# A row softmax: whole-tile passes, stores on Pool's queue, four tiles summed by DVE, instruction streams aligned

## Chip, cores, metric

One core of one Trainium2 chip. The metric is the device time of the kernel in microseconds; lower is better. "Landing" of a transfer is the last of the 16 semaphore updates that the trace has for it (512 for the 32 transfers of before). "Before" is the given kernel, "after" the changed one.

## The reference

```python
batch, seq, dim = 32, 512, 1024            # x is float32, temperature 0.5
scaled = x / temperature
shifted = scaled - np.max(scaled, axis=-1, keepdims=True)
exp_x = np.exp(shifted)
return (exp_x / np.sum(exp_x, axis=-1, keepdims=True)).astype(np.float32)
```

16384 rows of 1024 float32: 67.11 MB are read and 67.11 MB are written.

## The kernel before

Sixteen tiles of 128 partitions x 8 rows x 1024 elements (4 MiB), six buffers. SP issues loads, ACT issues stores; a load waits until the store that last used its buffer has landed (224.5 us in 10 waits, in the trace). Work goes in groups of four rows, two groups a tile, and DVE divides a group only after the maximum of the next one.

```python
TILES = [[8]] * 16
BUFS = 6
GROUP = 4
# ... (cut: pools, the list of groups)
def load():
    i = len(tiles)
    if i < len(TILES):
        xt = data.tile([P, sum(TILES[i]), d], f32, name="xt")
        nc.sync.dma_start(out=xt, in_=dram(xf, i))
        tiles.append(xt)

def maximum(g):            # DVE: top over 4 rows, bias = -scale * top
    ...
def exponential(g):        # ACT: one instruction per row, with its sum
    for b in range(k):
        nc.scalar.activation(row, row, Exp, bias=bias[:, b : b + 1], scale=scale,
                             accum_out=sums[:, b : b + 1])          # (shortened)

def divide(g):             # DVE
    nc.vector.reciprocal(recip, sums)
    for b in range(k):
        nc.vector.tensor_scalar_mul(row, in0=row, scalar1=recip[:, b : b + 1])

def store(g):              # after a tile's last group
    nc.scalar.dma_start(out=dram(of, i)[:, a : a + k, :], in_=tiles[i][:, a : a + k, :])
    load()

for _ in range(BUFS):
    load()
for g in range(len(groups) + 1):
    if g < len(groups):
        maximum(g)
        exponential(g)
    if g > 0:
        divide(g - 1)
        store(g - 1)
```

## Time and profile before

| | before |
|---|---|
| time, median of the first 3 runs | 318.26 us (317.97 to 318.32) |
| span of the profiled run | 316.0 us |
| first data packet, last data packet ends, last landing | 1.74, 314.80, 315.18 us |
| rate in the middle | 432 to 433 GB/s |

The last part of the page names each group of DMA issues: direction, issuing queue, count, size, and the median time from issue to landing.

```profile
xt<-in_x_dram SPq DMA_DIRECT2D x16, 4096.0 KB, 50.2
out_dram<-xt ACTq DMA_DIRECT2D x16, 4096.0 KB, 38.6
```

At 433 GB/s the bytes of a 4 MiB transfer alone take 9.7 us, so both queues are several transfers deep: the DMA engines (share 1.00 from 12.5 to 300 us), not DVE (busy 75% of the span) or ACT (47%), set the pace. The rest of the reading is in the prediction.

### The profile page before, as it was taken

What the parts mean: (1) busy time and instruction counts of PE and PEld (TensorE: products, weight loads), DVE (VectorE), ACT (ScalarE), POOL (GpSimd) and SP (SyncE); (2) the same over time, 40 slices, a digit from 0 to 9 for tenths busy, and PEclk for the clock granted to TensorE, in tenths of its full rate; (3) what the DMA queues carried; (4) which work ended last, traced back from release to release, by engine and by line L of the source; (5) the groups of instructions that cost most, each with busy time, mean ns of one, the idle gap of its engine ahead of it and who ended that gap; (6) DMA issues with size and microseconds to landing.
All of it is one profiled execution on the core that took longest, in us unless ns stands there. A gap on an engine that the chain in (4) does not pass through costs nothing.

```text
span 316.0 us, 620 instructions
## 1 busy us (share of the span) xinstructions
DVE 235.5 (75%) x224; ACT 149.6 (47%) x257; POOL 0.2 (0%) x4
## 2 busy tenths in 40 slices
DVE  0399999999689494994949859497693976949720
ACT  0176666666526255361554605546064560645500
POOL 0000000000000000000000000000000000000000
DMA  8999999999999999999999999999999999999996
GB/s 332 411 452 423 373 460 415 452 425 431 436 427 440 427 444 423 444 419 448 415 452 411 452 408 456 423 444 427 436 431 432 440 423 444 419 444 419 452 411 274
DMA packets 4612, 134.25 MB, mean 425 GB/s; under 512 B 512, under 2 KB 512, under 8 KB 512
## 3 DMA queue, kind: packets, MB, share of 16 engines
q1 hardware_dynamic: 2304, 67.11, 49.7%
q10 hardware_dynamic: 2304, 67.11, 49.2%
q14 instruction: 4, 0.03, 0.0%
HBM read 67.11 MB, written 67.11 MB: 425 GB/s over the span
## 4 chain that ended last, share of the span: by engine, by line
DVE 49%; DMA 32%; another core or an unknown queue 9%; ACT 5%; issue 1%; DVEq 0%; SPq 0%
DVE top L70 29%; DMA xt<-in_x_dram 20%; DVE xt L93 18%; DMA out_dram<-xt 12%; ACT xt L79 5%; DVE recip L91 1%; DVE bias L73 1%; DVEq L147 0%; SPq L61 0%
## 5 line engine op out<-in xcount | busy, mean ns | idle before, releaser
L79 ACT ACTIVATE xt<-xt,bias 128x1024 f32<-128x1024 f32 x128 | 145.4, 1137 | 136.8 <-DVE recip L91 119.4
L70 DVE TENSOR_REDUCE top<-xt 128x4 f32<-128x4096 f32 x32 | 141.3, 4416 | 62.6 <-DMA xt<-in_x_dram 62.6
L93 DVE TENSOR_SCALAR xt<-xt,recip 128x1024 f32<-128x1024 f32 x128 | 87.7, 749 | 1.1
L79 ACT ACTIVATION_READ_ACCUMULATOR xt<-xt,bias 128x1 f32 x128 | 23.9, 187 | 0.0
L79 ACT ACT_TABLE_LOAD x1 | 1.3, 1283 | 13.0 <-DMA xt<-in_x_dram 13.0
L91 DVE RECIPROCAL recip<-sums 128x4 f32<-128x4 f32 x32 | 5.5, 171 | 2.1 <-ACT xt L79 2.1
L73 DVE TENSOR_SCALAR bias<-top 128x4 f32<-128x4 f32 x32 | 5.4, 170 | 1.1
L133 POOL MEMSET const-bfloat16-1.0<- 128x1 bf16 x1 | 0.1, 101 | 0.0
L133 POOL MEMSET const-uint8-127<- 128x1 uint8 x1 | 0.1, 101 | 0.0
L133 POOL MEMSET const-float32-0.0<- 128x1 f32 x1 | 0.1, 98 | 0.2 <-issue 0.2
L133 POOL MEMSET const-float32-1.0<- 128x1 f32 x1 | 0.1, 98 | 0.0
## 6 DMA issues: line engine op xcount, KB each, us to landing
xt<-in_x_dram SPq DMA_DIRECT2D x16, 4096.0 KB, 50.2
out_dram<-xt ACTq DMA_DIRECT2D x16, 4096.0 KB, 38.6
```

The lines of the kernel that those rows point to most:

```text
L70: nc.vector.tensor_reduce(out=top, in_=tiles[i][:, a : a + k, :], axis=mybir.AxisListType.X, op=extreme)
L73: nc.vector.tensor_scalar_mul(bias, in0=top, scalar1=-scale)
L79: nc.scalar.activation(tiles[i][:, a + b, :], tiles[i][:, a + b, :], mybir.ActivationFunctionType.Exp, bias=bias[:, b : b + 1], scale=scal ...
L91: nc.vector.reciprocal(recip, sums)
L93: nc.vector.tensor_scalar_mul(tiles[i][:, a + b, :], in0=tiles[i][:, a + b, :], scalar1=recip[:, b : b + 1])
L133: nc = _bacc.Bacc("TRN2", target_bir_lowering=False, num_devices=1)
```

## The change

The intent: have DVE and ACT execute fewer instructions (209 instead of 240, 256 instead of 319) and align both streams, to be rid of the four instruction packets of 8 KB that the trace of before has in mid-run (two at 65.0 us, then 181.9 and 240.1); take the issuing of stores from ACT; and store the last tile in halves. To get ACT down, four tiles are summed by DVE, not by ACT's accumulator reads (0.19 us each, 128 before and 96 after).

```diff
-TILES = [[8]] * 16
+ROWS = 8
 BUFS = 6
-GROUP = 4
+PASSES = [[4, 4]] * 2 + [[8]] * 12 + [[4, 4]] * 2
+SUMMED = (3, 6, 9, 12)
...
-                accum_out=sums[:, b : b + 1],
+                **({} if i in SUMMED else dict(accum_out=sums[:, b : b + 1])),
...
+        if i in SUMMED:
+            nc.vector.tensor_reduce(
+                out=sums,
+                in_=tiles[i][:, a : a + k, :],
+                axis=mybir.AxisListType.X,
+                op=mybir.AluOpType.add,
+            )
         nc.vector.reciprocal(recip, sums)
...
-            nc.scalar.dma_start(out=dram(of, i)[:, a : a + k, :], in_=tiles[i][:, a : a + k, :])
-            if a + k == sum(TILES[i]):
-                load()
+        last = i == len(PASSES) - 1
+        if not last:
+            a, k = 0, a + k
+        if last or k == ROWS:
+            nc.gpsimd.dma_start(
+                out=dram(of, i)[:, a : a + k, :],
+                in_=tiles[i][:, a : a + k, :],
+                single_packet=True,
+            )
+            load()
...
     with tc.manual_schedule():
+        nc.vector.addr_align(128, offset=0, max_nops=0)
+        nc.scalar.addr_align(128, offset=0, max_nops=0)
```

With `max_nops=0` the padding in front of the aligned place is jumped over by a branch.

More of the change, by code (lines that the diff above doesn't have):

```diff
@@ L32 @@
     n, d = xf.shape
-    assert sum(sum(ks) for ks in TILES) * P == n
+    assert len(PASSES) * ROWS * P == n
     data = ctx.enter_context(tc.tile_pool(name="data", bufs=BUFS))
     stats = ctx.enter_context(tc.tile_pool(name="stats", bufs=4))
-    groups, first, r = [], [], 0
-    for i, ks in enumerate(TILES):
-        first.append(r)
-        r += sum(ks)
-        a = 0
-        for k in ks:
-            for b in range(0, k, GROUP):
-                m = min(GROUP, k - b)
-                groups.append((i, a + b, m, (a, k) if b + m == k else None))
-            a += k
+    groups = []
+    for i, ks in enumerate(PASSES):
+        assert sum(ks) == ROWS
+        for j, k in enumerate(ks):
+            groups.append((i, sum(ks[:j]), k))
     def dram(t, i):
-        k = sum(TILES[i])
-        block = t[P * first[i] : P * (first[i] + k), :]
-        return block.rearrange("(p k) d -> p k d", p=P, k=k)
+        block = t[P * ROWS * i : P * ROWS * (i + 1), :]
+        return block.rearrange("(p k) d -> p k d", p=P, k=ROWS)
     tiles, small = [], []
@@ L58, in load @@
         i = len(tiles)
-        if i < len(TILES):
-            xt = data.tile([P, sum(TILES[i]), d], f32, name="xt")
+        if i < len(PASSES):
+            xt = data.tile([P, ROWS, d], f32, name="xt")
             nc.sync.dma_start(out=xt, in_=dram(xf, i))
@@ L64, in maximum @@
     def maximum(g):
-        i, a, k, _ = groups[g]
+        i, a, k = groups[g]
         top, bias, sums, recip = (
@@ L75, in exponential @@
     def exponential(g):
-        i, a, k, _ = groups[g]
+        i, a, k = groups[g]
         bias, sums, _ = small[g]
@@ L84, in exponential @@
                 scale=scale,
-                accum_out=sums[:, b : b + 1],
+                **({} if i in SUMMED else dict(accum_out=sums[:, b : b + 1])),
             )
     def divide(g):
-        i, a, k, _ = groups[g]
+        i, a, k = groups[g]
         _, sums, recip = small[g]
+        if i in SUMMED:
[5 more added lines that the diff above has]
+            )
         nc.vector.reciprocal(recip, sums)
@@ L97, in store @@
     def store(g):
-        i, _, _, part = groups[g]
-        if part:
-            a, k = part
-            nc.scalar.dma_start(out=dram(of, i)[:, a : a + k, :], in_=tiles[i][:, a : a + k, :])
-            if a + k == sum(TILES[i]):
-                load()
+        i, a, k = groups[g]
+        last = i == len(PASSES) - 1
[8 more added lines that the diff above has]
+            load()
     with tc.manual_schedule():
+        nc.vector.addr_align(128, offset=0, max_nops=0)
+        nc.scalar.addr_align(128, offset=0, max_nops=0)
         for _ in range(BUFS):
```

## The prediction

Two terms of its sum are: +0.5 us for the issue of the last store by Pool, and -0.4 us for the overhead of a packet. With both the sum came to 318.3 - 1.3 + 0.5 - 0.4 = 317.1, and with the weight given to 319.2, to 317.3 us.

That loads and stores alternate by packets, each with about half, is in the trace of before: between 60 and 270 us 49.9% of the data packets are loads, and an engine changes from load to store or back at 87% of its packets (how engines are told apart comes under the result).

> **What bounds the kernel now.** I read the page first. Its second part says it at once: the 16 DMA engines are at nine tenths or more in every slice but the first and the last, while DVE has 75% of the span and ACT 47%.
>
> ```profile
> span 316.0 us, 620 instructions
> DVE 235.5 (75%) x224; ACT 149.6 (47%) x257; POOL 0.2 (0%) x4
> DMA  8999999999999999999999999999999999999996
> q1 hardware_dynamic: 2304, 67.11, 49.7%
> q10 hardware_dynamic: 2304, 67.11, 49.2%
> q14 instruction: 4, 0.03, 0.0%
> ```
>
> The loads (q1) and the stores (q10) together fill 98.9% of 16 engines' time. Which rate is that? I asked for stretches; the last two columns are the DMA share and GB/s.
>
> ```profile
> core 0: us, DVE busy (x) ACT busy (x) POOL busy (x), PEclk, DMA share, GB/s
> 0.00:12.50 12.50, 0.00 (x0) 0.00 (x0) 0.20 (x4) 1.00 0.92 372
> 12.50:32.00 19.50, 18.69 (x16) 12.63 (x20) 0.00 (x0) 1.00 1.00 434
> 32.00:40.00 8.00, 7.93 (x9) 5.25 (x11) 0.00 (x0) 1.00 1.00 389
> 40.00:160.00 120.00, 101.83 (x98) 63.86 (x111) 0.00 (x0) 1.00 1.00 432
> 160.00:282.00 122.00, 89.39 (x86) 58.55 (x102) 0.00 (x0) 1.00 1.00 433
> 282.00:300.00 18.00, 15.30 (x16) 9.27 (x16) 0.00 (x0) 1.00 1.00 433
> 300.00:316.00 16.00, 2.35 (x4) 0.00 (x0) 0.00 (x0) 1.00 0.80 344
> ```
>
> The same 433 GB/s stands whether only loads run (12.5 to 32), both (40 to 282) or only stores (282 to 300). In the trace's records of single packets nearly every 32 KB packet takes 1.213 us, load or store. This is a ceiling, and 134.22 MB over it take 309.8 us. Everything else is small: the first packet starts at 1.74 us and is about 0.7 us slow; at 34 to 37 us, as the first store begins, load packets take 1.3 to 2.6 us, about 0.8 us an engine; then 309.8 + 1.7 + 0.7 + 0.8 = 313.0. Most engines indeed end between 313.0 and 313.8, two later, the last at 314.8. The span ends 1.2 us after that, and the timed run is 318.26 - 316.0 = 2.3 us longer than the profiled span.
>
> The chain of waits names DVE for 49%, but that is not the bound: until 77 us DVE works without a gap, and yet DMA is full. The waits show the slack.
>
> ```profile
> ACT xt L79 <- DVE recip L91: 119.4, 25, 7.9
> DVE top L70 <- DMA xt<-in_x_dram: 62.6, 12, 13.0
> SPq L61 <- DMA out_dram<-xt: 224.5, 10, 53.8
> ```
>
> (Engine waiting, what for: us in all, times, longest.) DVE waits for data, ACT for DVE, and the load queue for stores to free one of 6 buffers.
>
> [...]in mixed stretches each side gets about half[...]. [...]the trace shows 8 KB fetch packets, four within the span (two near 65 us, at 182 and at 240), each of 0.31 us, next to a data packet lengthened by 0.3 to 0.5 us.[...]
>
> **The change part by part.**
>
> *Traffic.* Neither bytes nor loads change. The floor stays 309.8 us, and nothing that DVE or ACT save counts by itself.
>
> *Passes.* Twelve tiles get one maximum of 128x8192 in place of two of 128x4096 (4.416 us, of which 4096 elements at 0.96 a ns are 4.27): 0.15 us saved per tile, and with one multiply of bias and one reciprocal less (0.17 each) about 0.4 us a tile, 5 us of DVE in all. DVE works beside the transfers, so worth 0. The price is latency: a division now stands behind an 8.6 us maximum, not a 4.4 us one. Store 1 goes out near 51.6 instead of 47.4, and store 2 near 66.0 instead of 62.2. With six loads (58 us of transfer) queued at the start, no engine runs dry from that.
>
> *Summed tiles.* In four tiles 8 accumulator reads of 0.187 us each leave ACT (4 x 1.5 = 6 us) and DVE gains a sum of 8.6 us each, 34 us. DVE then has about 235.5 - 5 + 34 = 265 us, still under 310. Locally a summed tile takes DVE 8.8 (maximum and bias) + 8.6 (sum) + 5.6 (reciprocal and 8 x 0.69) = 23.0 us against 19.4 us of DMA per tile, a normal one 14.4; an average of 16.6 keeps up.
>
> *Instructions.* ACT falls from 257 busy instructions to 225, DVE from 224 to 24 + 128 + 20 + 20 = 192. If no block is fetched inside the span, four packets go, and the two late engines at the end with them. The end then falls toward the bulk's 313.2 to 313.8: a gain of 1.0 to 1.6 us.
>
> *Pool's queue.* ACT stops waiting for divisions; it had 47% and it is worth 0. Pool issues a store at the end of a division.[...]
>
> *Last tile in two halves.* Before, the store queue never ran dry at the end (433 GB/s until 300, full until about 313), so halves gain nothing there; they only protect against a gap.
>
> *One packet per store.* The step I am least sure of. If the whole share of an engine, 8 x 32 KB, is one packet, stores get eight turns to a load's one: a store would land about 11 us after its issue, not 38.6. No backlog of stores is then left for the end. Worked through by the row durations, with landing of tile 13 (counted from 0) as zero: the engines have loads 14, 15 and store 11 to do, until 29; store 12, a summed tile, is issued at about 4.7 + 23.0 = 27.7 and keeps them till 38.7; store 13 is issued at 27.7 + 4.6 + 5.6 = 37.9, till 48.4; store 14 only at 37.9 + 14.8 = 52.7. That is 4.3 us of idle engines; then the halves of 15 arrive in time. If instead packets alternate one to one as before, about one store's backlog (9.7 us) bridges this.
>
> *Sum.* Alternating: 318.3 - 1.3 (fetches, late engines)[...] = 317.1. Store-first: 317.1 + 4.3 = 321.4 at worst, less whatever backlog is left; I take half, 319.2. The summed tiles and the packing were presumably placed for a reason, so I weigh the first at nearly nine in ten: **317.3 us**.
>
> **Rivals.** (1) Store-first packets open gaps at the end: 319 to 321.4. For it: packet-wise turns; against: six buffers, and 28 us between the last division (282 if it never waited) and the DMA's end. (2) Stores of Pool's queue run slower, by smaller packets[...]: were each store packet 3% slower, that is 155 x 0.03 = 4.6 us, near 322; nothing in the profile before speaks for it or against it. (3) The slowdown at 34 to 37 us vanishes too, and all engines end together: 313.0 - 0.8 + 1.2 + 2.3 = 315.7. (4) The transfers hide everything: 318.3.
>
> **Range and chances.** Faster by 2% means under 311.9, below 309.8 + 1.74 + 2.3 = 313.8 even with no idle at all: it needs a rate above 433, which no stretch shows, so 2%. Slower by 2% means over 324.6, which takes rival 2 with over 4% on stores, or both of the first two: 4%. The rest, 94%. Range 315.2 to 320.8: rival 3 below, most of rival 1 above.
>
> **What would show it.** Right: 432 to 434 GB/s in the middle; no instruction packets in the span; DVE near 265 us and still waiting for loads; last store landing about 1 us earlier than before. The time from issue to landing of stores decides the packing: near 38 us alternation, near 11 us store-first, and then DMA slices under nine tenths after 280 us would show the gap. Wrong: a middle under 425 GB/s (stores slower), many more packets on the store queue, or DVE without waits from 90 us on.

## The result

After: 319.21 us (318.50 to 319.69, 6 runs); before, in the same rounds: 318.09 us (317.96 to 318.32, 6 runs). Ratio 1.0031, 95% interval 1.0016 to 1.0047. Ratios here are the mean time of one kernel's fast runs over that of the other's of the same rounds, so not quite the ratio of the medians. It is the same within 2%, and 1 us slower beyond the noise; inside the predicted range, but on the other side of before than the point of 317.3.

The page after, the parts that answer to those shown for before: span, busy time, DMA share in 40 slices, queues, and DMA issues with their median time to landing.

```profile
span 316.7 us, 563 instructions
...
DVE 265.4 (84%) x192; ACT 145.3 (46%) x225; POOL 9.4 (3%) x21
...
DMA  8999999999999999999999999999999999999995
...
q1 hardware_dynamic: 2304, 67.11, 49.5%
q0 software_dynamic: 2448, 67.11, 49.1%
q14 instruction: 4, 0.03, 0.0%
...
xt<-in_x_dram SPq DMA_DIRECT2D x16, 4096.0 KB, 48.4
out_dram<-xt POOLq DMA_DIRECT2D x15, 4096.0 KB, 25.7
out_dram<-xt POOLq DMA_DIRECT2D x2, 2048.0 KB, 12.0
```

Three things to see. DVE has 30 us more work and no cost of it shows: the engines of the DMA are as full as before (a share of 1.00 from 40 to 300 us in both). The store queue is now the software one (q0), with the same bytes. And q14 still counts four instruction packets: the fetches, which the change was made to avoid, are all there.

By stretches (last columns: DMA share, GB/s), the ceiling is the same.

```profile
40.00:160.00 120.00, 112.51 (x73) 58.47 (x90) 3.19 (x6) 1.00 1.00 433
160.00:282.00 122.00, 108.28 (x79) 57.38 (x89) 3.72 (x7) 1.00 1.00 434
282.00:300.00 18.00, 15.95 (x17) 12.43 (x22) 1.06 (x2) 1.00 1.00 431
```

The waits after: Pool waits for divisions, DVE waits less for loads (33.9 us, 62.6 before), SP still waits for stores to land (225.6 us in 10 waits).

```profile
POOL out_dram L107 <- DVE xt L96: 294.1, 17, 33.4
...
DVE top L66 <- DMA xt<-in_x_dram: 33.9, 8, 13.9
```

So where is 1 us? Not in the transfers as a body. The landing times of loads and stores in the two traces lie within 2 us of each other and come together towards the end: the last load lands at 282.6 before and 281.3 after, the store of the fourteenth tile at 295.9 and 295.8. What differs is at the two ends of the program.

**The closing.** In the profiled runs the last landing is at 315.18 before and 315.20 after, but the span ends at 315.99 and 316.70: 0.81 us against 1.50 us after the landing. (The trace of after is from one of its faster runs: its span of 316.7 us stands against a mean of 317.2.) The closing instructions, by engine, are these (duration in ns as least, median, most; then when the first and last began). Before:

```profile
L147 SPq EVENT_SEMAPHORE  x7: 17/28/28, 270.5 to 315.9; - x7
L147 POOLq EVENT_SEMAPHORE  x4: 17/17/17, 315.4 to 315.9; - x4
L147 POOLq DRAIN  x3: 34/41/70, 0.7 to 315.7; - x3
```

After:

```profile
L159 SPq EVENT_SEMAPHORE  x11: 17/28/4426, 310.4 to 316.6; - x11
L159 POOLq EVENT_SEMAPHORE  x4: 17/17/17, 316.0 to 316.6; - x4
L159 POOLq DRAIN  x3: 34/101/12747, 303.2 to 316.4; - x3
```

Pool's drain, 70 ns at most before, begins at 303.2 as the last store is issued and takes 12,747 ns, until 315.94. That is 0.74 us after the last store landed. SP was ready for the closing barrier at 315.39, and Pool let it pass at 315.98; before it passed at 315.35, 0.03 us after SP was ready. In this trace a store on Pool's queue that lands last therefore costs the barrier 0.6 us, and a short drain and the clearing of semaphores behind it another 0.1 us (0.10 and 0.14 us for drain and clearing, 0.07 and 0.09 before).

**The late DMA engines.** The records of single DMA packets carry no engine number, but they can be chained: each is put behind the packet whose end is nearest before its start. This gives 16 chains. Before, each has exactly 256 packets of 32 KB; after, each has 248 of 32 KB and 16 of 16 KB, which are the half stores of the last tile. When they end (us), with the instruction fetches that fall into the chain:

```text
before   middle engine 313.29   third last 313.82
         314.42  fetches at 65.0 and 181.9
         314.80  fetches at 65.0 and 240.1
after    middle engine 313.18   third last 313.54
         313.85  fetches at 1.77 and 162.1
         314.86  fetches at 4.03 and 207.7
```

In each kernel, the engines that end last are the ones that carried the fetches, one engine for ACT's and one for DVE's (told apart by the instruction counts below). (The one at 1.77 came before its engine's first data packet, so no chain leads to it; the engine of the fetch at 162.1 is the one that got its first packet latest, at 2.81 us. That it carried both is inferred.) A fetch in mid-run takes 0.31 us itself (the two early ones took 1.04 and 0.33 us), and the data packet behind it 0.11 to 0.54 us longer. Before, DVE's engine lost about 0.7 us by its first fetch and 0.85 by its second against the middle one. The last landing waits for it.

The change moved the fetches instead of removing them. Counted in the trace, ACT executes 319 instructions before and fetches about its 67th and 194th, 127 apart; after, it executes 256, jumps at its third to the aligned place, fetches for the jump, and again at about its 134th, 131 further. DVE's two stand 139 apart before (47th and 186th) and 126 after (3rd and 129th). From these distances I estimate that a packet of 8 KB brings about 128 instructions; by that estimate a stream of 209 or 256 needs one in mid-run at least, wherever it starts. The fetch for DVE's jump came at 4.03 us, behind a first data packet; its engine was then 0.93 us behind the middle one, and still 1.0 us at 197 us, before its second fetch.

One more loss shows in other traces of this kind. With e4 and e8, below, the engine of the fetch near 4 us is also 0.8 us behind at first, but at 36 to 38 us, where the first store begins and load packets are slow on all engines, it loses another 0.5 us, and ends 2.0 and 2.1 us behind the middle one instead of 1.7. In the trace of after it lost nothing there. So how late this engine ends differs by 0.4 us from trace to trace, for a reason that stays open.

### The profile page after: what moved, and what is told of

Read it like the earlier page. It is cut to its first block, busy times and chain, and to the rows that moved or that the text cites. A ratio compares the mean times of both kernels' runs of the same rounds, so it can differ in the third digit from the quotient of the medians.

```text
span 316.7 us, 563 instructions
## 1 busy us (share of the span) xinstructions
DVE 265.4 (84%) x192; ACT 145.3 (46%) x225; POOL 9.4 (3%) x21
## 4 chain that ended last, share of the span: by engine, by line
issue 89%; DMA 4%; POOL 3%; POOLq 0%
DMA xt<-in_x_dram 4%; POOL out_dram L107 3%; POOLq L159 0%; POOLq L107 0%
## 5 line engine op out<-in xcount | busy, mean ns | idle before, releaser
L75 ACT ACTIVATE xt<-xt,bias 128x1024 f32<-128x1024 f32 x128 | 142.6, 1135 | 140.8 <-DVE bias L69 125.4
L66 DVE TENSOR_REDUCE top<-xt 128x8 f32<-128x8192 f32 (+1 forms) x20 | 139.5, 6976 | 33.9 <-DMA xt<-in_x_dram 33.9
L96 DVE TENSOR_SCALAR xt<-xt,recip 128x1024 f32<-128x1024 f32 x128 | 86.6, 749 | 0.7
L88 DVE TENSOR_REDUCE sums<-xt 128x8 f32<-128x8192 f32 x4 | 34.7, 8678 | 0.0
L75 ACT ACTIVATION_READ_ACCUMULATOR xt<-xt,bias 128x1 f32 x96 | 17.9, 186 | 0.0
L107 POOL DMA_DIRECT2D out_dram<-xt x17 | 9.2, 539 | 294.1 <-DVE xt L96 294.1
L94 DVE RECIPROCAL recip<-sums 128x8 f32<-128x8 f32 (+1 forms) x20 | 3.8, 188 | 2.2 <-ACT xt L75 2.1
L69 DVE TENSOR_SCALAR bias<-top 128x8 f32<-128x8 f32 (+1 forms) x20 | 3.4, 171 | 0.7
## 6 DMA issues: line engine op xcount, KB each, us to landing
out_dram<-xt POOLq DMA_DIRECT2D x15, 4096.0 KB, 25.7
```

The costliest lines, as they stand in the source:

```text
L66: nc.vector.tensor_reduce(out=top, in_=tiles[i][:, a : a + k, :], axis=mybir.AxisListType.X, op=extreme)
L69: nc.vector.tensor_scalar_mul(bias, in0=top, scalar1=-scale)
L75: nc.scalar.activation(tiles[i][:, a + b, :], tiles[i][:, a + b, :], mybir.ActivationFunctionType.Exp, bias=bias[:, b : b + 1], scale=scal ...
L88: nc.vector.tensor_reduce(out=sums, in_=tiles[i][:, a : a + k, :], axis=mybir.AxisListType.X, op=mybir.AluOpType.add,)
L96: nc.vector.tensor_scalar_mul(tiles[i][:, a + b, :], in0=tiles[i][:, a + b, :], scalar1=recip[:, b : b + 1])
L107: nc.gpsimd.dma_start(out=dram(of, i)[:, a : a + k, :], in_=tiles[i][:, a : a + k, :], single_packet=True,)
```

## The experiments

Twelve kernels, five rounds each; each against before on the same chip. The main theory had two halves. A: Pool's drain holds the closing barrier, +0.6 us. F: the DMA engines that carry fetches end last, and where the fetches fall decides how late. Rivals: B, stores of the software queue are slower or later; C, passes, sums or packing cost the time.

| run | time (us) | ratio to before | 95% interval | last landing to end of span (us) |
|---|---|---|---|---|
| e1_pool_only | 318.12 | 1.0005 | 0.9993 to 1.0017 | 1.46 |
| e2_align_only | 317.80 | 0.9992 | 0.9979 to 1.0005 | 0.81 |
| e3_no_align | 318.36 | 1.0013 | 1.0001 to 1.0024 | 1.50 |
| e4_last_sp | 318.43 | 1.0015 | 0.9999 to 1.0031 | 1.25 |
| e5_thin | 316.84 | 0.9966 | 0.9948 to 0.9984 | 0.81 |
| e6_dve_short | 317.72 | 0.9993 | 0.9974 to 1.0012 | 0.81 |
| e7_no_sum | 318.94 | 1.0019 | 1.0006 to 1.0032 | 1.50 |
| e8_no_packet | 319.27 | 1.0037 | 1.0019 to 1.0054 | 1.49 |
| e9_align_delay | 317.56 | 0.9984 | 0.9972 to 0.9996 | 0.81 |
| e10_sp_delay | 320.14 | 1.0059 | 1.0046 to 1.0071 | 0.85 |
| e11_after_again | 319.23 | 1.0034 | 1.0022 to 1.0046 | 1.50 |
| e12_after_delay | 318.42 | 1.0010 | 0.9997 to 1.0024 | 1.50 |

Before had a median of 317.94 to 318.11 us. Each run's span is known, but only one run's trace is kept, and it was often the slowest of the five; where that matters I use the mean span of all runs less the last column. This is an estimate: it takes the closing of the one trace for that of all runs. For before, the mean of 316.2 less 0.81 gives a last landing at 315.4 on average.

### Stores on Pool's queue alone

```diff
-            nc.scalar.dma_start(out=dram(of, i)[:, a : a + k, :], in_=tiles[i][:, a : a + k, :])
+            nc.gpsimd.dma_start(out=dram(of, i)[:, a : a + k, :], in_=tiles[i][:, a : a + k, :])
```

> The kernel before with its 16 stores issued by Pool, nothing else. Theory A (Pool's closing drain ends about 0.75 us after the last landing and holds the closing barrier, +0.6 us): ratio about 1.002, last landing unchanged near 315.2, drain end near 315.9, span 316.5 to 316.8. Rival B (stores of the software queue are slower or later): last landing itself 1 us or more later than 315.2. Rival C (passes, sums, packing or alignment make the loss): ratio 1.000.

The closing is as A has it: 1.46 us, drain until 315.80 against a last landing at 315.10. Here SP is no earlier than Pool: its first closing wait is for the last store, and its list of the others, 0.06 us each, comes behind it and ends at 315.73.

```profile
L147 SPq EVENT_SEMAPHORE  x11: 17/28/28, 315.1 to 316.5; - x11
...
L147 POOLq DRAIN  x3: 34/101/14485, 301.3 to 316.3; - x3
```

But the time is only 0.18 us above before by the medians, not 0.6. Mean span 316.38 less 1.46 puts the average last landing at 314.9, half a microsecond earlier than before's. The fetches are the same four; in this trace the packets behind them were lengthened by 1.28 us in all, in that of before by 1.80. Three of those here were stores, all four there were loads, and over all the traces lengthened loads and stores overlap (0.24 to 0.54 and 0.11 to 0.43 us). So B is refuted, the longer closing is shown, and why the landing came earlier stays open. The drain alone is not shown as its cause here: Pool lets the barrier pass at 315.85, only 0.1 us after SP's own list.

### The alignment alone

```diff
+        nc.vector.addr_align(128, offset=0, max_nops=0)
+        nc.scalar.addr_align(128, offset=0, max_nops=0)
         for _ in range(BUFS):
             load()
```

> The kernel before with the two alignments added alone. Theory A2 (the alignment is a jump to a block that has to be fetched when the loads already run; it moves fetches to 1.8 to 4 us, and doesn't lessen them): 5 or 6 fetch packets in the span against 4 before, and the engines that carry them end last, 0.3 to 1 us later than 314.8; ratio 1.001 to 1.003, with more spread from run to run than before's 0.4 us. Rival C2 (alignment is free): fetches at most 4, ratio 1.000.

Five fetches, as expected: at 1.75 and 4.10 us, then 124.95, 163.21 and 253.65. The cost isn't there: 317.80 us, equal to before. The profiled run, the slowest of five, had its last landing at 315.69; the mean of all is 316.06 - 0.81 = 315.25. So the expected loss is refuted: alignment adds a fetch, but by itself no time that I can measure. The traced slowest run has its last engine 1.8 us behind the middle one, before's trace 1.5; the other four runs must have had less. One reading that would fit: with the alignment DVE fetches twice, at 4.10 and 163.21, and before it fetched twice as well; the fifth fetch is ACT's, whose engine ended 0.4 us before DVE's in the trace of before. The chains of this trace change places, so this isn't shown.

### The changed kernel without the alignment

```diff
-        nc.vector.addr_align(128, offset=0, max_nops=0)
-        nc.scalar.addr_align(128, offset=0, max_nops=0)
```

> The changed kernel without the two alignments. Theory A2: fetches near 1.8 and 4 us are gone; with first block crossings near instruction 47 of DVE and 67 of ACT as before, still two on each engine (209 and 255 instructions), so 4 in the span; ratio about 1.002 (the drain's 0.6 us remains), spread of times under 0.5 us. If alignment is what saves fetches: 5 or more, and slower than the changed kernel's 1.0031.

1.0013 (expected 1.002). Four fetches, at 56.6, 90.0, 229.0 and 285.5 us, as expected: no fewer and no more than with the alignment. The spread was 0.9 us, not under 0.5. Against the changed kernel's 1.0031 and 1.0034 alignment would cost some 0.6 us there, though the intervals overlap, while alone it cost none. The last experiment comes back to it.

### The last tile stored by SP

```diff
-            nc.gpsimd.dma_start(
+            issuer, packing = (nc.sync, {}) if last else (nc.gpsimd, dict(single_packet=True))
+            issuer.dma_start(
                 out=dram(of, i)[:, a : a + k, :],
                 in_=tiles[i][:, a : a + k, :],
-                single_packet=True,
+                **packing,
             )
```

> The changed kernel with the last tile's two half stores issued by SP, so that Pool's last store lands some 10 us before the end. Theory A: Pool's drain ends near 306 and the closing barrier follows the last landing within 0.2 us; ratio about 0.6/318 lower than the changed kernel's 1.0031, so near 1.0012. Rival B or C: no change against 1.0031.

1.0015, near the expected 1.0012. The drain ends at 308.46, 7 us ahead of the last landing at 315.69, so Pool no longer holds the barrier.

```profile
L160 SPq EVENT_SEMAPHORE  x11: 17/28/28, 303.8 to 316.9; - x11
...
L160 POOLq DRAIN  x3: 34/93/17037, 291.4 to 316.7; - x3
```

Yet the closing took 1.25 us and not 0.9: a wait took the drain's place. SP now waits for the last store among its first closing waits, and its remaining ones, at 0.06 us each, begin at 315.71 and end at 316.14. What was removed from one engine came back for two thirds on another. The six runs fell into two clusters, spans of 315.8 to 316.1 and 316.9 to 317.4, so only part of the ratio's fall is this.

### No fetch at all, with a wrong result

```diff
-        nc.vector.tensor_reduce(...)              # maximum, and the bias
-        for b in range(k):
-            nc.scalar.activation(..., bias=bias[:, b : b + 1], accum_out=sums[:, b : b + 1])
+        nc.scalar.activation(whole, whole, mybir.ActivationFunctionType.Exp, scale=scale)
-        nc.vector.reciprocal(recip, sums)
-        for b in range(k):
-            nc.vector.tensor_scalar_mul(...)
+        nc.vector.tensor_scalar_mul(whole, in0=whole, scalar1=0.5)
```

> Wrong results on purpose: the kernel before with one exponential and one multiply per tile and no maximum or sum, the same 32 transfers on the same queues; DVE and ACT have under 50 instructions. Theory F (the two engines that carry instruction fetches end 1.0 us after the rest, so fetches cost 1.0 us of the end): no fetch in the span, all 16 DMA engines end within 0.8 us, last landing near 314.2 instead of 315.2, ratio 0.997. Rival: the late engines are late for another reason: the last landing stays near 315.2, ratio 1.000.

This is the clearest of the twelve. Its output is wrong (there is no normalisation), its 32 transfers are those of before. Its queues, without any line of instruction packets, and its rate in the middle:

```profile
DMA packets 4608, 134.22 MB, mean 426 GB/s; under 512 B 512, under 2 KB 512, under 8 KB 512
...
q1 hardware_dynamic: 2304, 67.11, 49.8%
q10 hardware_dynamic: 2304, 67.11, 49.3%
```

All 16 chains end between 313.05 and 313.83 us, the middle one at 313.18; the last landing is at 314.18, where 314.2 was expected. Ratio 0.9966, expected 0.997. DVE works 71 us here instead of 235 and ACT 114 instead of 150, and yet the middle engine ends within 0.1 us of before's: the transfers set the time. (One of six runs was a microsecond slower, 318.29.) So fetches cost before 1.0 us of its time (315.18 against 314.18), by way of two DMA engines.

### One fetch of DVE fewer

```diff
+PASS = [8] * 14 + [4] * 2
+WIDE = (2, 4, 6, 8, 10)
...
+        if i in WIDE:
+            whole = tiles[i][:, a : a + k, :]
+            nc.vector.tensor_tensor(out=whole, in0=whole,
+                in1=recip.unsqueeze(2).to_broadcast([P, k, d]), op=mybir.AluOpType.mult)
+            return
```

> The kernel before with whole-tile passes in 14 tiles and one broadcast multiply in 5 of them: DVE has some 163 instructions instead of 240, so it crosses one block and not two, ACT is unchanged. Theory F: three fetches in the span; DVE's DMA engine ends near 313.9, ACT's stays last near 314.4; last landing 0.2 to 0.5 us earlier, ratio 0.9985 to 0.9995. Rival: 1.000 or above.

Three fetches, at 56.7, 136.5 and 185.5, as expected; the last landing was 0.2 us earlier than before's in the trace, and the ratio is 0.9993. One run of 319.46 widens the interval, which includes 1. In this trace some engines to which I could chain no fetch also ended between 314.2 and 314.7, and several store packets were lengthened together at 56 us, so the picture isn't clean. Inconclusive.

### The changed kernel without the sums on DVE

```diff
-SUMMED = (3, 6, 9, 12)
+SUMMED = ()
```

> The changed kernel with all sums by ACT: ACT has 288 instructions, DVE 205. Theory A: the sums only take DVE's slack; the ratio is 1.003 as for the changed kernel, or up to 0.001 more if ACT[...] fetches once more. DVE's waits for loads rise from 34 us to some 65. Rival C (the sums delay stores and cost time): ratio falls by 0.002 or more.

1.0019; five fetches instead of four; DVE's waits for loads rise to what was expected.

```profile
DVE top L66 <- DMA xt<-in_x_dram: 67.7, 13, 13.6
```

The interval (1.0006 to 1.0032) overlaps that of the changed kernel, and the rival's fall of 0.002 is not reached: the sums take DVE's slack and I can't show that they take time. Nor do they save it.

### The changed kernel without the packing

```diff
-                single_packet=True,
```

> The changed kernel without one packet per store. Theory A: packing changes neither the turns of the queues nor the landing times; ratio 1.003, stores land 25 us after issue (median), packets of 32 KB. Rival (packing matters): stores land in a different time, ratio differs from 1.003 by over 0.002.

1.0037, the same four fetches within 0.6 us, stores of 32 KB packets (as with the packing), landing after 25.7 us as in the changed kernel.

```profile
q0 software_dynamic: 2448, 67.11, 49.0%
...
out_dram<-xt POOLq DMA_DIRECT2D x15, 4096.0 KB, 25.7
```

Packing does nothing here that the trace can show. The 25.7 us against before's 38.6 come from later issue of the stores (the fifth at 106.5 instead of 95.6 us, the tenth at 207.3 instead of 192.9), not from any precedence on the engines: between 60 and 270 us the chained engines change from load to store or back at 87% of their packets, in the traces of before, of after and of this run alike.

### Both early fetches ahead of the data

Before, with the alignment and SP's first load delayed by four drains:

```diff
+        nc.vector.addr_align(128, offset=0, max_nops=0)
+        nc.scalar.addr_align(128, offset=0, max_nops=0)
+        for _ in range(4):
+            nc.sync.drain()
         for _ in range(BUFS):
             load()
```

> The kernel before with the two alignments and four drains ahead of SP's first load, so that both fetches of the jump reach their DMA engines before the first data packets do (in the changed kernel ACT's did, at 1.76 us, and cost its engine 0.1 to 0.3 us; DVE's came behind a data packet, at 4.02, and cost 0.9). Theory F: the loads start 0.1 to 0.3 us later, both early fetches stand before 2.1 us, DVE's DMA engine then loses only its later fetch (0.7 to 0.85 us), ACT's its two later ones (1.0); last landing near 314.9, ratio 0.998 to 0.9995. Rival (the place of the fetch doesn't matter): 0.999 to 1.001, the delay added.

SP issues its first load at 0.94 us instead of 0.73, the fetches stand at 1.78 and 1.89 us, and the first data packet at 1.92. All later times in this trace are thus 0.2 us later than they would be, and still the last landing is at 315.02, the last engine 1.24 us behind the middle one instead of 1.51. Time 317.56 us against 317.97, ratio 0.9984, spread 0.3 us: 0.4 us faster than before, and the interval excludes 1. It is the fastest kernel with a right result, faster than both, if by little. Against the alignment alone (0.9992) the intervals overlap. The last landing came 0.1 us later than expected, the ratio where it was expected.

### All stores on SP, and the same delay

```diff
-            nc.gpsimd.dma_start(
+            nc.sync.dma_start(
...
-                single_packet=True,
             )
-            load()
+            if i > 1:
+                load()
```

(in the changed kernel, with the four drains as above.)

> The changed kernel with all stores issued by SP (a load follows two stores later), no packing, and the same four drains: no Pool drain at the end, two early fetches ahead of the data, one later fetch on each of the two engines. Theory A and F together: last landing near 314.6, the span ends 0.8 us after it, ratio 0.996 to 0.998, faster than both kernels. Rival (one queue for loads and stores opens gaps): DMA share under 1.00 in the middle and a ratio over 1.000.

My expectation fell: 320.14 us. There is no drain to wait for and the middle is full, but with loads and stores in one queue three engines end late, the last at 318.5 us, while 13 end by 314.0.

```profile
160.00:282.00 122.00, 107.04 (x76) 55.84 (x86) 0.00 (x0) 1.00 1.00 431
282.00:300.00 18.00, 15.92 (x18) 10.47 (x19) 0.00 (x0) 1.00 1.00 430
300.00:320.00 20.00, 0.96 (x2) 0.00 (x0) 0.00 (x0) 1.00 0.69 295
```

The rival, gaps in the middle, is wrong too: the DMA share is 1.00 there. From 98 us on this trace has single packets lengthened by 0.1 to 0.9 us about every 19 us, once for each change from loads to stores, in which the other traces have none. That a late engine meets each change alone, and is made later by it, would fit; I have not shown it.

### The changed kernel again

No edit; a control on the chip of the two runs above.

> The changed kernel once more, on the same chip as the two above: ratio 1.0016 to 1.0047 as before. Theory A and F: span ends 1.5 us after the last landing; the last engine is the one that fetched near 4 us and near 208 us, 1.6 to 2.1 us behind the middle one.

1.0034, as the first time. The span ends 1.50 us after the last landing, which is at 315.80 in this trace. Its fetches stand at 1.80, 3.75, 163.5 and 208.3; the last engine ends 2.3 us behind the middle one, more than the expected 2.1. In this trace the chains change places once, so that I can't assign the fetch at 3.75.

### The changed kernel with the delay

```diff
         nc.scalar.addr_align(128, offset=0, max_nops=0)
+        for _ in range(4):
+            nc.sync.drain()
```

> The changed kernel with the same four drains ahead of SP's first load, nothing else. Theory F: DVE's first fetch then stands before the data and costs its DMA engine 0 to 0.3 us instead of 0.9; the last engine ends near 314.2 to 314.6 instead of 314.9 to 315.5, the span still ends 1.5 us after the last landing; ratio 1.0005 to 1.0020 against the changed kernel's 1.0031 and 1.0034. Rival (the place of the first fetch isn't what makes the changed kernel's transfers end later than before's): ratio 1.003 or above.

1.0010: the changed kernel becomes 0.7 us faster by a start that is 0.2 us later. The fetches stand at 1.76 and 1.92 us, ahead of the data. DVE's engine, with a later fetch at 207 us, ends at 314.46, 0.96 us behind the middle one, where the trace of after has 1.68 and others of its kind 2.1. The last landing is at 314.79. The closing still takes 1.50 us, and that is why it is no faster than before. Two limits: this run and the control above are from different chips, compared by way of before on each; and the drains without the alignment were not run, so that an effect of the later start itself is not excluded.

## Why the prediction was right, and where not

The measured 319.21 us lies in 315.2 to 320.8, and "within 2%" was given 94%. The reason for that was right: the ceiling of 433 GB/s stayed (431 to 434 after), so 30 us of additional DVE work and some 4 us less ACT work moved nothing. But the point of 317.3 was 1.9 us off and on the other side of before; that the range held in spite of it owes to its width of 5.6 us. By its terms:

- **Instructions, -1.3 us: failed.** The step said that if no block is fetched inside the span, four packets go and the late engines with them. What such a removal is worth was right: 1.0 us in the run without fetches. But four fetches stayed, two of them moved to the start. The condition was taken from the words of the change and not worked out: before's trace already showed 8 KB packets, and fetches 127 ACT instructions apart, a spacing at which a stream of 256 could be expected to fetch in mid-run once. On average the last landing came 0.3 us later than before's (mean span 317.2 less 1.50, against 315.4), not 1.3 us earlier. DVE's early fetch behind the first data is the reason that the runs support: ahead of the data, the changed kernel is 0.7 us faster, with the limits named at that run.
- **Pool's queue, +0.5 us: right in size, wrong in cause.** The lead of the last store isn't seen: its issue comes at 303.2 instead of 302.4, and the engines still have earlier stores to do. Nor is a later start of the packets clear in the traces: the first packet of the first store comes 4.3 us after its issue by Pool (5.2 us in the run with Pool's queue alone), and 4.5 us after that by ACT before. In this trace DVE runs a maximum (at 9 of the 17 issues) or nothing while Pool issues; an issue beside other work of DVE was not tested. What costs is the closing drain, 0.7 us, of which the prediction had no word.
- **A packet's overhead, -0.4 us: failed.** Store packets take 1.213 us as before, with the packing or without.
- **One packet per store.** The first branch, alternation, was the right one: no idle engines after 280 us (DMA share 1.00 from 282 to 300). That the other branch's 319.2 equals the measured time is chance: its gap of 4.3 us isn't there. The test named for it was poor: "near 38 us alternation, near 11 us store-first", and the answer was 25.7. Later issue and hence a shorter queue, of which the same text had worked out the times (51.6 and 66.0 us for stores 1 and 2; 52.9 and 67.2 measured), gave that without any change of turns; the order of the packets in the traces and the run without packing tell it.
- **Passes and summed tiles, worth 0: right.** DVE's 265.4 us were predicted as 265; a maximum over 8192 elements took 8.68 us against 2 x 4.41, the difference of 4096 elements 4.27 us (0.96 elements a ns), as the text had it. The named sign "no instruction packets in the span" came out wrong, and told at once which step had failed.
- **Two slips without weight.** From 282 to the DMA's end at 313 are 31 us, not 28. And the profiled run itself took 317.86 us, so a run is 1.9 us longer than its span, not 2.3; 318.26 was the median of other runs.

The sum as measured: closing +0.7 and last landing +0.3 on average, together the 1.0 us between the mean spans (the second term is what the first leaves, not measured apart). Of the rivals, (1), (2) and (3) did not happen, though the time falls into the range of (1), and (4), that transfers hide everything, was nearest in mechanism.

## What to carry to other kernels

DMA was full from end to end (a share of 1.00 from 40 to 300 us, before and after), and only its slowest engine (1.5 us behind the middle one before, 1.7 after) and the closing (0.81 and 1.50 us) made a difference: look at how far apart the 16 engines end, at what each late one carried, and at what runs between the last landing and the end. In these traces DVE's fetch left its DMA engine 0.4 us behind the middle one when it came before the first data (e12), and 0.9 us when it came behind it (after); count the instruction packets (four before, four after, five with the alignment alone) before you pay for fewer instructions. And look at who waits for the last store: Pool's drain ended 0.70 us (e1) and 0.74 us (after) behind the last landing and held the barrier for 0.6 us (after), but moving the last tile to SP won back only 0.25 us of the closing's 0.69, since SP's list of waits took the drain's place.
